# Output projection: a ninth of sixteen row-block pairs by seven products, final norm weights applied at the end, residual of three double groups added by DMA

## Chip, cores, metric

One core of one Trainium2 chip. The metric is the device time of one execution in microseconds (us), the median of several runs. The profile is of one execution, with the times of every instruction of the engines PE (matrix products), DVE (vector), ACT (scalar), POOL (GpSimd) and SP (which issues most DMAs).

## What is computed

One layer of a hybrid decoder for 256 tokens and 4096 channels, in float32. The normalised input is multiplied by one large input matrix, three branches (convolution, spatial gating, pooling) work on the parts, and their results, side by side, are `y`, 256 x 4096. The change is in what follows:

```python
    y = jnp.concatenate([ya, yb, yc], axis=-1) @ w_out[l]
    x = x + y
return _rmsnorm(x, final_g)      # x * rsqrt(mean(x*x) + eps) * final_g
```

So each output row needs its residual `x`, the sum of squares of the whole row, and at last a factor per row and a weight per column.

## The kernel before

Every float32 product is made from two parts of each operand: ACT casts a weight tile to a high part (line 237, `w_hi`), DVE subtracts it from the raw tile for a low part (line 238, `w_lo`), and PE does three matmuls of 128 x 128 x 512 for each block (high x high, high x low, low x high: lines 904 to 906 in the output projection, 357 to 359 elsewhere). A split tile has 1024 columns; five such slots go round, and PE uses a tile two tiles after it was split (`AHEAD`).

The output projection is the last stage. Its 4096 columns are done as four double groups of 1024 (`paired_columns`, g = 0, 2, 4, 6). The 4096 rows of `w_out` are 16 blocks p of 256 rows, taken in the order of `ORDER` (`LAST_ORDER` in the last double group). A block that is not in `PAIRED` ("plain") makes eight products: two token halves c, two column halves h, two row halves j. That is 24 matmuls from two split tiles. A block in `PAIRED` is done as a 2 x 2 x 2 block product by seven products, 21 matmuls, with sums of token blocks that were prepared before (`combos`) and sums of weight blocks that DVE makes on the way (lines 984, 987, 988, `w_sums`). It takes four splits with 3584 columns in all, in the order of products (1, 2), (3), (5, 7), (6, 4). The products add up in PSUM banks q1 to q8 over all 16 blocks.

When the last paired block of a double group is done, `between` combines q1, q5, q6 and q7 with one ACT copy and eight DVE sums of 512 columns, into the rows `xn`, which already hold the residual (`load_rows` loads it by SP at the fifth block of each double group, with 512 weights of the final norm for each half, `fg_bc`). When a bank of the plain products q2, q3, q4, q8 is complete, `rows_done` adds it to `xn` on DVE (line 893), ACT squares and sums the row (line 894) and DVE multiplies the norm weights in (line 899).

In the last double group the last five split tiles are held, and the second token half's products on them come last (30 matmuls). While these run, the first token half's rows are finished: `finish_rows` makes the row factor from the mean (DVE and ACT, lines 1022 to 1026), DVE multiplies the rows by it in five pieces (line 1031; the last 512 columns with their norm weights, line 1034), and SP writes each piece out (line 1035). Then the same is done for the second half.

The framework lists each engine's instructions itself: of those it thinks ready, the one written first goes first. So neighbouring instructions stand in an order a little different from the program's. Three raw tiles of 1 MB (`raw_tile`, tag `raw`) and two tiles of 4 x 512 columns (`scratch`, tag `sums`) go round in the last stage.

Of the kernel before, what the change touches and what calls it, by code (L numbers as in the profile page):

```python
# [28 lines left out]
P = 128  # L29
# [50 lines left out]

PAIRED = [5, 6, 7, 8, 9, 10, 11, 13]
ORDER = [0, 5, 1, 6, 2, 7, 8, 3, 9, 4, 10, 11, 12, 13, 14, 15]
LAST_ORDER = [0, 5, 1, 6, 2, 7, 8, 3, 9, 10, 4, 11, 13, 12, 14, 15]


PN = 0
# [9 lines left out]
def trunk(ctx: ExitStack, tc: tile.TileContext, x, xt, params, w1, wv, w2, w_pw, w_c, w_o, wst, bbias, blg, blb, fg, out):  # L98
# [777 lines left out]
        nc.scalar.activation(out=ssq[:, 0, 8:9], in_=ones[:, :1], func=AF.Sqrt)  # L876

    LAST = D - 512
    fg_bc = {}

    def load_rows(c0):
        at = len(traced())
        fg_bc[c0] = outp.tile([P, 512], F32, tag="fg", name="fg_bc", bufs=2)
        nc.sync.dma_start(out=fg_bc[c0], in_=fg[c0 : c0 + 512].partition_broadcast(P))
        nc.sync.dma_start(out=xn[:, :, c0 : c0 + 512], in_=x[:, c0 : c0 + 512].rearrange("(c p) d -> p c d", p=P))
        for ins in traced()[at:]:
            if ins.engine == mybir.EngineType.SP:
                tc.add_manual_dep(ins, last_load[0].name, ISSUE_ORDER, reason="behind the weights")

    def add_rows(c, ps, c0, w, i):  # L890

        z = xn[:, c, c0 : c0 + w]
        nc.vector.tensor_tensor(out=z, in0=ps, in1=z, op=ALU.add)  # L893
        nc.scalar.activation(out=ps, in_=z, func=AF.Square, accum_out=ssq[:, c, i : i + 1])
        return z

    def rows_done(c, ps, c0):
        z = add_rows(c, ps, c0, 512, c0 // 512)
        nc.vector.tensor_tensor(out=z, in0=z, in1=fg_bc[c0], op=ALU.mult)

    def product(q, a, w, j, f, l):

# [7 lines left out]
    def paired_columns(g, last=False):  # L910
# [18 lines left out]
        def plain(p, h, w):  # L929
            if (p, h) in holds:  # L930
                held.append((p, h, w))
            for c in range(1 if held else 2):
                for j in range(2):
                    into(PLAIN[c][h], y_hl[2 * p + j][:, c], w, j)
                if p == order[-1] and not held:
                    rows_done(c, q[PLAIN[c][h]], (g + h) * 512)

        def seven(p, products, w):
            i = PAIRED.index(p)
# [7 lines left out]
        def between():  # L947

            s = scratch("c_sums")
            v, y = s[:, 0], s[:, 1]  # L950
            x11, x12 = [xn[:, 0, (g + h) * 512 : (g + h + 1) * 512] for h in range(2)]
            x21, x22 = [xn[:, 1, (g + h) * 512 : (g + h + 1) * 512] for h in range(2)]
            nc.scalar.copy(out=v, in_=q[1])
            nc.vector.tensor_tensor(out=x11, in0=q[1], in1=x11, op=ALU.add)
            nc.vector.tensor_tensor(out=v, in0=q[6], in1=v, op=ALU.subtract)
            nc.vector.tensor_tensor(out=y, in0=q[5], in1=v, op=ALU.add)
            nc.vector.tensor_tensor(out=v, in0=q[7], in1=v, op=ALU.add)
            nc.vector.tensor_tensor(out=x22, in0=q[7], in1=x22, op=ALU.add)
            nc.vector.tensor_tensor(out=x21, in0=x21, in1=v, op=ALU.subtract)
            nc.vector.tensor_tensor(out=x12, in0=x12, in1=y, op=ALU.add)  # L960
            nc.vector.tensor_tensor(out=x22, in0=x22, in1=y, op=ALU.add)

        for n, p in enumerate(order):
            if g == 0 and n == 2:
                branches_done()
            if n == 4:
                load_rows(g * 512)
                load_rows((g + 1) * 512)
            raw = raw_tile("w_raw")
            for h in range(2):  # L970
                at = ((g + h) * 8 + p // 2) * P * 2048
# [21 lines left out]
            feed(*split(flat[:, 1024:]), lambda a, b, p=p: seven(p, (6, 4), (a, b)))  # L993
        if not last:
            return
        drain()
        rows_done(0, q[2], D - 1024)
        mean = mean_so_far(0, 7)
        add_rows(0, q[3], LAST, 512, 7)
        finish_rows(0, mean, 7, [1024, 1024, 1024, 512, 512])  # L1000
        for h in range(2):
            parts = [(p, w) for p, i, w in held if i == h]
            out_q = q[PLAIN[1][h]]
# [4 lines left out]
                rows_done(1, out_q, D - 1024)  # L1008
        mean = mean_so_far(1, 7)
        add_rows(1, out_q, LAST, 512, 7)  # L1010
        finish_rows(1, mean, 7, [512, 1024, 1024, 1024, 512])

    def mean_so_far(c, n):
        a = fin.tile([P, 1], F32, tag="fin_a", name="fin_a", bufs=2)
# [4 lines left out]
    def finish_rows(c, mean, i, pieces):  # L1019

        a, y, s = [fin.tile([P, 1], F32, tag=f"fin_{n}", name=f"fin_{n}", bufs=2) for n in "mys"]
        nc.vector.tensor_scalar(out=a, in0=ssq[:, c, i : i + 1], scalar1=1.0 / D, scalar2=mean, op0=ALU.mult, op1=ALU.add)
        nc.scalar.activation(out=s, in_=a, func=AF.Sqrt)
        nc.vector.reciprocal(out=y, in_=s)
        nc.vector.tensor_scalar(out=s, in0=y, scalar1=y, scalar2=a, op0=ALU.mult, op1=ALU.mult)
        nc.vector.tensor_scalar(out=s, in0=s, scalar1=-0.5, scalar2=1.5, op0=ALU.mult, op1=ALU.add)
        at = 0
        for w in pieces:
            z = xn[:, c, at : at + w]
            if at < LAST:  # L1030
                nc.vector.tensor_scalar(out=z, in0=z, scalar1=y, scalar2=s, op0=ALU.mult, op1=ALU.mult)  # L1031
            else:
                nc.vector.tensor_tensor(out=y, in0=y, in1=s, op=ALU.mult)
                nc.vector.scalar_tensor_tensor(out=z, in0=z, scalar=y, in1=fg_bc[LAST], op0=ALU.mult, op1=ALU.mult)
            nc.sync.dma_start(out=out[c * P : (c + 1) * P, at : at + w], in_=z)
            at += w

# [87 lines left out]
```

## Time and profile before

| | us |
|---|---|
| median of 3 runs | 1365.07 (1365.01 to 1366.15) |
| the profiled execution | 1364.61 |
| its span, first to last instruction | 1362.9 |
| output projection, first to last matmul | about 1022.6 to 1351.1 |

The span lies 1.7 us below the time of its execution, and that execution 0.5 us below the median. Of the span PE is busy for 99%, DVE for 78%, ACT for 51%; POOL for almost nothing. The page's second part shows PE at nine tenths or more in all but the last of 40 slices, at full granted clock, and DVE at nine tenths from slice 32 to the end.

### The profile page before, as it was taken

Reading aid. Unit: us, or ns where it says so; the run is one execution under the profiler, and the core shown is the slowest. Engines: PE = TensorE matmul, PEld = TensorE weight load, DVE = VectorE, ACT = ScalarE, POOL = GpSimd, SP = SyncE. Lnnn points to the kernel's source line nnn. Section 1 sums busy time; section 2 is a strip of 40 time slices with the busy share of each in tenths; the row PEclk is TensorE's granted clock in tenths of the full one; section 3 lists DMA queues with packets and bytes.
Section 4 is the critical chain, followed back from the end, with each engine's and each line's share of the span. In section 5 each row is a group of like instructions: output and inputs, shape, how many; then the busy total and the mean of one; then the engine's idle time right before and its main releaser. Section 6 shows DMA issues by size and latency. Waiting matters only on the chain.

```text
span 1362.9 us, 16202 instructions
## 1 busy us (share of the span) xinstructions
PE 1349.2 (99%) x6104; PEld 1120.1 (82%) x6104; DVE 1058.8 (78%) x1491; ACT 692.0 (51%) x837; POOL 5.8 (0%) x52
## 2 busy tenths in 40 slices
PE   9999999999999999999999999999999999999996
PEld 7888888888988888888888888888888888888885
DVE  7558888888888888777445844456878999999998
ACT  7653444435445434554344434446755665666563
POOL 0000000000000000000000000000000000000000
PEclk9999999999999999999999999999999999999998
DMA  9975555555556555555555555554736676666764
GB/s 333 351 263 192 198 185 187 193 193 199 185 200 196 195 203 187 186 187 187 182 185 186 190 202 195 185 189 147 248 123 233 217 251 216 221 223 213 243 220 156
DMA packets 58895, 281.01 MB, mean 206 GB/s; under 512 B 8896, under 2 KB 12352, under 8 KB 35520
## 3 DMA queue, kind: packets, MB, share of 16 engines
q1 hardware_dynamic: 58672, 279.95, 59.0%
q8 instruction: 48, 0.79, 0.2%
q14 instruction: 31, 0.25, 0.1%
q10 hardware_dynamic: 144, 0.02, 0.0%
HBM read 275.75 MB, written 4.19 MB: 205 GB/s over the span
## 4 chain that ended last, share of the span: by engine, by line
PE 97%; DVE 1%; DMA 1%; issue 0%; ACT 0%; SPq 0%; DVEq 0%
PE q L358 24%; PE q L359 24%; PE q L357 24%; PE q L905 8%; PE q L904 8%; PE q L906 8%; DMA gb<-in_blb_dram 1%; DMA x_raw<-in_xt_dram 0%; DVE xn L1031 0%; PE q L410 0%; PE q L632 0%; PE q L334 0%; DVE w_lo L238 0%; PE q L783 0%; DVE xn L893 0%
## 5 line engine op out<-in xcount | busy, mean ns | idle before, releaser
L238 DVE TENSOR_TENSOR w_lo<-w_raw,w_hi 128x1024 fp32r<-128x1024 f32 (+1 forms) x495 | 584.2, 1186 | 266.3 <-ACT w_hi L237 264.2
L237 ACT CAST w_hi<-w_raw 128x1024 fp32r<-128x1024 f32 (+1 forms) x495 | 501.8, 1023 | 528.2 <-PE q L359 306.6
L357 PE MATMUL q<-w_hi,act 128*128 128x512 f32 (+2 forms) x1504 | 578.9, 386 | 0.3 <-ACT act L314 0.3
L358 PE MATMUL q<-w_lo,act 128*128 128x512 f32 (+2 forms) x1504 | 577.4, 384 | 0.7 <-DVE w_lo L238 0.7
L359 PE MATMUL q<-w_hi,act 128*128 128x512 f32 (+2 forms) x1504 | 577.5, 384 | 0.0
L358 PEld LDWEIGHTS q<-w_lo,act 128*128 128x128 f32 x1504 | 282.9, 188 | 56.7 <-DVE w_lo L238 1.9
L359 PEld LDWEIGHTS q<-w_hi,act 128*128 128x128 f32 x1504 | 282.7, 188 | 55.3
L357 PEld LDWEIGHTS q<-w_hi,act 128*128 128x128 f32 x1504 | 282.8, 188 | 55.2 <-ACT act L314 0.8
L544 DVE SCALAR_TENSOR_TENSOR c_a<-h_a,par,c_a 128x256 f32<-128x256 f32 x360 | 153.6, 478 | 0.0
L905 PE MATMUL q<-w_lo,act 128*128 128x512 f32 x384 | 149.6, 390 | 0.0
L906 PE MATMUL q<-w_hi,act 128*128 128x512 f32 x384 | 149.3, 390 | 0.0
L904 PE MATMUL q<-w_hi,act 128*128 128x512 f32 x384 | 147.9, 390 | 0.0
L237 ACT CAST w_hi<-w_sums 128x1024 fp32r<-128x1024 f32 x64 | 67.4, 1053 | 71.9 <-DVE w_sums L988 44.3
L905 PEld LDWEIGHTS q<-w_lo,act 128*128 128x128 f32 x384 | 72.1, 188 | 15.5 <-DVE w_lo L238 0.5
L904 PEld LDWEIGHTS q<-w_hi,act 128*128 128x128 f32 x384 | 71.9, 188 | 15.3 <-ACT w_hi L237 0.4
L906 PEld LDWEIGHTS q<-w_hi,act 128*128 128x128 f32 x384 | 72.1, 188 | 14.9
L238 DVE TENSOR_TENSOR w_lo<-w_sums,w_hi 128x1024 fp32r<-128x1024 f32 x64 | 77.8, 1218 | 3.3 <-ACT w_hi L237 2.8
L984 DVE TENSOR_TENSOR w_sums<-w_raw 128x1024 f32<-128x1024 f32 x32 | 39.0, 1218 | 1.6 <-DMA w_raw<-in_w_o_dram 1.5
L905 PE MATMUL q<-w_lo,combo 128*128 128x512 f32 x96 | 37.6, 391 | 0.0
L906 PE MATMUL q<-w_hi,combo 128*128 128x512 f32 x96 | 37.4, 389 | 0.0
L904 PE MATMUL q<-w_hi,combo 128*128 128x512 f32 x96 | 37.4, 389 | 0.0
L988 DVE TENSOR_TENSOR w_sums<-w_sums,w_raw 128x512 f32<-128x512 f32 x32 | 21.9, 684 | 0.1
(143 smaller groups left out, 489.9 us busy)
## 6 DMA issues: line engine op xcount, KB each, us to landing
w_raw<-in_w_dram SPq DMA_DIRECT2D x149, 1024.0 KB, 4.8
w_raw<-in_w_o_dram SPq DMA_DIRECT2D x128, 512.0 KB, 4.9
w_raw<-in_wv_dram SPq DMA_DIRECT2D x20, 1024.0 KB, 4.8
w_raw<-in_w_pw_dram SPq DMA_DIRECT2D x9, 1024.0 KB, 4.9
x_rows<-in_x_dram SPq DMA_DIRECT2D x4, 1024.0 KB, 6.8
xn<-in_x_dram SPq DMA_DIRECT2D x8, 512.0 KB, 6.5
out_dram<-xn SPq DMA_DIRECT2D x6, 512.0 KB, 3.3
w_raw<-in_w_dram SPq DMA_DIRECT2D x5, 512.0 KB, 5.6
```

The lines of the kernel that those rows point to most:

```text
L237: nc.scalar.copy(out=hi[:, w], in_=raw[:, w])
L238: nc.vector.tensor_tensor(out=lo[:, w], in0=raw[:, w], in1=f32(hi[:, w]), op=ALU.subtract)
L357: nc.tensor.matmul(ps[:, :w], lhsT=act[:, c, 0], rhs=hi, start=f, stop=False)
L358: nc.tensor.matmul(ps[:, :w], lhsT=act[:, c, 0], rhs=lo, start=False, stop=False)
L359: nc.tensor.matmul(ps[:, :w], lhsT=act[:, c, 1], rhs=hi, start=False, stop=l)
L544: nc.vector.scalar_tensor_tensor(out=c_a[:, m], in0=src, scalar=w, in1=c_a[:, m], op0=ALU.mult, op1=ALU.add)
L904: nc.tensor.matmul(q, lhsT=a[:, 0], rhs=hi, start=f, stop=False)
L905: nc.tensor.matmul(q, lhsT=a[:, 0], rhs=lo, start=False, stop=False)
L906: nc.tensor.matmul(q, lhsT=a[:, 1], rhs=hi, start=False, stop=l)
L984: nc.vector.tensor_tensor(out=w57, in0=w[:, 0::3], in1=w[:, 2:3].broadcast_to([P, 2, 512]), op=ALU.add)
L988: nc.vector.tensor_tensor(out=s[:, 3], in0=s[:, 2], in1=w[:, 1], op=ALU.add)
```

## The change

- A ninth block, p = 12, is done by seven products in each double group. `ORDER` and `LAST_ORDER` are written anew: there are now seven plain blocks, and most paired blocks stand two in a row; in the last double group 11, 12 and 13 stand three in a row.
- The norm weights are no longer loaded for each half and multiplied in group by group. All 4096 are loaded in two DMAs of 1 MB into raw tiles behind the last weights, and `finish_rows` multiplies row factor and weights in by one scalar_tensor_tensor for each piece. The pieces are now 512, 512, 1024, 1024, 1024 for the first half and 512, 512, 1024, 1024, 512, 512 for the second.
- In the first three double groups the residual is no longer loaded into `xn`. `between` makes the combinations without it (two ACT copies, four DVE sums), `columns_done` adds each plain bank to them with one DVE sum, and POOL then issues a DMA that adds the residual from memory onto `xn` (four of 256 KB a double group). The squares of these rows are taken at the fourth block of the next double group, out of SBUF, into a `scratch` tile.
- In the last double group the residual is loaded and added as before.

```diff
-PAIRED = [5, 6, 7, 8, 9, 10, 11, 13]
-ORDER = [0, 5, 1, 6, 2, 7, 8, 3, 9, 4, 10, 11, 12, 13, 14, 15]
-LAST_ORDER = [0, 5, 1, 6, 2, 7, 8, 3, 9, 10, 4, 11, 13, 12, 14, 15]
+PAIRED = [5, 6, 7, 8, 9, 10, 11, 12, 13]
+ORDER = [0, 5, 1, 6, 7, 2, 8, 9, 3, 10, 11, 4, 12, 13, 14, 15]
+LAST_ORDER = [0, 5, 6, 1, 7, 8, 2, 9, 10, 3, 11, 12, 13, 4, 14, 15]
...
-    def load_rows(c0):
+    def load_rows(c0, residual):
         at = len(traced())
-        fg_bc[c0] = outp.tile([P, 512], F32, tag="fg", name="fg_bc", bufs=2)
-        nc.sync.dma_start(out=fg_bc[c0], in_=fg[c0 : c0 + 512].partition_broadcast(P))
-        nc.sync.dma_start(out=xn[:, :, c0 : c0 + 512], in_=x[:, c0 : c0 + 512].rearrange("(c p) d -> p c d", p=P))
+        if residual:
+            nc.sync.dma_start(out=xn[:, :, c0 : c0 + 512], in_=x[:, c0 : c0 + 512].rearrange("(c p) d -> p c d", p=P))
...
     def rows_done(c, ps, c0):
-        z = add_rows(c, ps, c0, 512, c0 // 512)
-        nc.vector.tensor_tensor(out=z, in0=z, in1=fg_bc[c0], op=ALU.mult)
+        add_rows(c, ps, c0, 512, c0 // 512)
...
                 if p == order[-1] and not held:
-                    rows_done(c, q[PLAIN[c][h]], (g + h) * 512)
+                    columns_done(c, h)
...
             nc.scalar.copy(out=v, in_=q[1])
-            nc.vector.tensor_tensor(out=x11, in0=q[1], in1=x11, op=ALU.add)
+            if last:
+                nc.vector.tensor_tensor(out=x11, in0=q[1], in1=x11, op=ALU.add)
+            else:
+                nc.scalar.copy(out=x11, in_=q[1])
+                y = x12
             nc.vector.tensor_tensor(out=v, in0=q[6], in1=v, op=ALU.subtract)
             nc.vector.tensor_tensor(out=y, in0=q[5], in1=v, op=ALU.add)
             nc.vector.tensor_tensor(out=v, in0=q[7], in1=v, op=ALU.add)
...
+            else:
+                nc.vector.tensor_tensor(out=x22, in0=q[7], in1=y, op=ALU.add)
+                z21.append(v)
...
+        def columns_done(c, h):
+
+            c0 = (g + h) * 512
+            z, r = xn[:, c, c0 : c0 + 512], q[PLAIN[c][h]]
+            if (c, h) == (1, 0):
+                nc.vector.tensor_tensor(out=z, in0=r, in1=z21[0], op=ALU.subtract)
+            else:
+                nc.vector.tensor_tensor(out=z, in0=r, in1=z, op=ALU.add)
+            nc.gpsimd.dma_start(out=z, in_=x[c * P : (c + 1) * P, c0 : c0 + 512], accum_op=ALU.add)
+            late_squares.append((c, c0))
+
         for n, p in enumerate(order):
...
+            while n == 3 and late_squares:
+                c, c0 = late_squares.popleft()
+                junk = scratch("junk")[:, 0]
+                nc.scalar.activation(out=junk, in_=xn[:, c, c0 : c0 + 512], func=AF.Square, accum_out=ssq[:, c, c0 // 512 : c0 // 512 + 1])
             if n == 4:
-                load_rows(g * 512)
-                load_rows((g + 1) * 512)
+                load_rows(g * 512, last)
+                load_rows((g + 1) * 512, last)
...
+        for at in (0, 2048):
+            fg_bc.append(raw_tile("fg_bc"))
+            nc.sync.dma_start(out=fg_bc[-1], in_=fg[at : at + 2048].partition_broadcast(P))
+            tc.add_manual_dep(traced()[-1], last_load[0].name, ISSUE_ORDER, reason="in the order of use")
...
-        finish_rows(0, mean, 7, [1024, 1024, 1024, 512, 512])
+        finish_rows(0, mean, 7, [512, 512, 1024, 1024, 1024])
...
-        finish_rows(1, mean, 7, [512, 1024, 1024, 1024, 512])
+        finish_rows(1, mean, 7, [512, 512, 1024, 1024, 512, 512])
...
+        nc.vector.tensor_tensor(out=y, in0=y, in1=s, op=ALU.mult)
         at = 0
         for w in pieces:
             z = xn[:, c, at : at + w]
-            if at < LAST:
-                nc.vector.tensor_scalar(out=z, in0=z, scalar1=y, scalar2=s, op0=ALU.mult, op1=ALU.mult)
-            else:
-                nc.vector.tensor_tensor(out=y, in0=y, in1=s, op=ALU.mult)
-                nc.vector.scalar_tensor_tensor(out=z, in0=z, scalar=y, in1=fg_bc[LAST], op0=ALU.mult, op1=ALU.mult)
+            g = fg_bc[at // 2048][:, at % 2048 : at % 2048 + w]
+            nc.vector.scalar_tensor_tensor(out=z, in0=z, scalar=y, in1=g, op0=ALU.mult, op1=ALU.mult)
             nc.sync.dma_start(out=out[c * P : (c + 1) * P, at : at + w], in_=z)
             at += w
```

## Rows read from the trace of the kernel before

**Rows 1.** The page, part 1 (busy us, share, instructions) and part 4 (chain).

```profile
PE 1349.2 (99%) x6104; PEld 1120.1 (82%) x6104; DVE 1058.8 (78%) x1491; ACT 692.0 (51%) x837; POOL 5.8 (0%) x52
...
PE 97%; DVE 1%; DMA 1%; issue 0%; ACT 0%; SPq 0%; DVEq 0%
```

**Rows 2.** Waits from 1000 to 1365 us: who waited for whom, total us, times, longest.

```profile
ACT w_hi L237 <- PE q L906: 53.7, 59, 2.6
...
DVE w_sums L984 <- DMA w_raw<-in_w_o_dram: 1.5, 2, 0.9
PEld q L905 <- DVE w_lo L238: 1.1, 3, 0.5
```

**Rows 3.** Timeline of PE: start us, us, engine, line; last double group's ends.

```profile
1269.15 0.39 PE L904 MATMUL q<-w_hi,act 128*128 128x512 f32 x1
...
1271.87 0.39 PE L904 MATMUL q<-w_hi,act 128*128 128x512 f32 x1
...
1350.89 0.39 PE L906 MATMUL q<-w_hi,act 128*128 128x512 f32 x1
```

**Rows 4.** Windows of 10 us: busy us (instructions) by engine, PEclk, DMA share, GB/s.

```profile
1310.00:1320.00 10.00, 10.00 (x46) 8.29 (x45) 10.00 (x11) 7.49 (x9) 0.00 (x0) 1.00 0.57 202
...
1340.00:1350.00 10.00, 9.97 (x45) 7.83 (x44) 8.66 (x18) 2.37 (x7) 0.00 (x0) 1.00 0.01 2
```

**Rows 5.** Groups by line and form, 1000 to 1365 us (busy us, mean ns, idle before).

```profile
L238 DVE TENSOR_TENSOR w_lo<-w_raw,w_hi 128x1024 fp32r<-128x1024 f32 x100 | 119.6, 1219 | 11.2 <-ACT w_hi L237 10.5
...
L984 DVE TENSOR_TENSOR w_sums<-w_raw 128x1024 f32<-128x1024 f32 x32 | 39.0, 1218 | 1.6 <-DMA w_raw<-in_w_o_dram 1.5
```

**Rows 6.** Timeline of DVE, three neighbours inside a paired block.

```profile
1326.58 1.22 DVE L238 TENSOR_TENSOR w_lo<-w_raw,w_hi 128x1024 fp32r<-128x1024 f32 x1
1327.72 0.68 DVE L987 TENSOR_TENSOR w_sums<-w_sums,w_raw 128x512 f32<-128x512 f32 x1
1328.32 0.68 DVE L238 TENSOR_TENSOR w_lo<-w_raw,w_hi 128x512 fp32r<-128x512 f32 x1
```

**Rows 7.** Timeline of DVE around and in the last double group.

```profile
1254.84 1.23 DVE L238 TENSOR_TENSOR w_lo<-w_raw,w_hi 128x1024 fp32r<-128x1024 f32 x1 [1.49 <-ACT w_hi L237]
...
1271.19 0.68 DVE L893 TENSOR_TENSOR xn<-q,xn 128x512 f32<-128x512 f32 x1
...
1301.86 1.22 DVE L238 TENSOR_TENSOR w_lo<-w_sums,w_hi 128x1024 fp32r<-128x1024 f32 x1
...
1341.28 2.35 DVE L238 TENSOR_TENSOR w_lo<-w_raw,w_hi 128x1024 fp32r<-128x1024 f32 x2
```

**Rows 8.** Timeline of DVE, the end: rows of both token halves finished.

```profile
1348.48 2.71 DVE L1031 TENSOR_SCALAR xn<-xn,fin_y,fin_s 128x1024 f32<-128x1024 f32 x4
...
1351.85 0.68 DVE L893 TENSOR_TENSOR xn<-q,xn 128x512 f32<-128x512 f32 x1
1352.44 0.74 DVE L1034 SCALAR_TENSOR_TENSOR xn<-xn,fin_y,fg_bc 128x512 f32<-128x512 f32 x1
1353.11 0.14 DVE L1016 TENSOR_SCALAR fin_a<-fin_a 128x1 f32<-128x1 f32 x1
...
1354.54 2.71 DVE L1031 TENSOR_SCALAR xn<-xn,fin_y,fin_s 128x512 f32<-128x512 f32 x4
...
1357.48 0.75 DVE L1034 SCALAR_TENSOR_TENSOR xn<-xn,fin_y,fg_bc 128x512 f32<-128x512 f32 x1
```

**Rows 9.** Timeline of SP: the last output DMA's issue.

```profile
1358.26 0.52 SPq L1035 DMA_DIRECT2D out_dram<-xn  x1
```

**Rows 10.** Windows of 2 us, columns as in rows 4.

```profile
1357.00:1359.00 2.00, 0.00 (x0) 0.00 (x0) 1.16 (x3) 0.00 (x0) 0.00 (x0) 0.50 1.02 408
```

**Rows 11.** The page, part 6: DMA issues, count, KB each, median us to landing.

```profile
xn<-in_x_dram SPq DMA_DIRECT2D x8, 512.0 KB, 6.5
...
fg_bc<-in_fg_dram SPq DMA_DIRECT2D x8, 256.0 KB, 4.5
...
out_dram<-xn SPq DMA_DIRECT2D x4, 256.0 KB, 3.1
```

More of the change, by code (lines that the diff above doesn't have):

```diff
@@ L878, in trunk @@
     LAST = D - 512
-    fg_bc = {}
-    def load_rows(c0):
+    fg_bc = []
+    late_squares = deque()
+    def load_rows(c0, residual):
         at = len(traced())
-        fg_bc[c0] = outp.tile([P, 512], F32, tag="fg", name="fg_bc", bufs=2)
-        nc.sync.dma_start(out=fg_bc[c0], in_=fg[c0 : c0 + 512].partition_broadcast(P))
-        nc.sync.dma_start(out=xn[:, :, c0 : c0 + 512], in_=x[:, c0 : c0 + 512].rearrange("(c p) d -> p c d", p=P))
+        if residual:
+            nc.sync.dma_start(out=xn[:, :, c0 : c0 + 512], in_=x[:, c0 : c0 + 512].rearrange("(c p) d -> p c d", p=P))
         for ins in traced()[at:]:
@@ L957, in between @@
             nc.vector.tensor_tensor(out=v, in0=q[7], in1=v, op=ALU.add)
[L958 to L961, printed above, removed]
+            if last:
+                nc.vector.tensor_tensor(out=x22, in0=q[7], in1=x22, op=ALU.add)
+                nc.vector.tensor_tensor(out=x21, in0=x21, in1=v, op=ALU.subtract)
+                nc.vector.tensor_tensor(out=x12, in0=x12, in1=y, op=ALU.add)
+                nc.vector.tensor_tensor(out=x22, in0=x22, in1=y, op=ALU.add)
+            else:
+                nc.vector.tensor_tensor(out=x22, in0=q[7], in1=y, op=ALU.add)
+                z21.append(v)
+        z21 = []
+        def columns_done(c, h):
[7 more added lines that the diff above has]
+            late_squares.append((c, c0))
         for n, p in enumerate(order):
```

## Prediction

> **What bounds the kernel now.** I read the page first: PE is busy for 99% of the span and carries 97% of the chain that ended last; POOL does almost nothing [rows 1]. The waits say whether PE is ever short of work in the last stage: of its waits only 1.1 us, three times, are for a split tile (w_lo), while ACT waits 53.7 us for PE to free a slot [rows 2]. PE's own timeline gives the price of a matmul: twelve between 1269.15 and 1271.87, so 0.2267 us, and the last double group's 360 take 1269.15 to about 1351.1, 0.4 us more than 360 x 0.2267 [rows 3]. So what leaves PE leaves the span, if nothing takes its place. The windows name what may: DVE is busy 10.00 of 10 us at 1310, and PE is still whole there; in 1340 to 1350, at the end of the loop, it is 9.97 [rows 4]. Two engines run level, and the change moves work between them.
>
> **PE.** A seventh product instead of an eighth saves 3 matmuls a double group, 12 in all: 12 x 0.2267 = -2.72 us. That is the whole of what the change can take from PE.
>
> **DVE's budget.** A split of 1024 columns and the first weight sum take 1.22 us each [rows 5], but start 1.14 us apart, and ones of 512 columns 0.60 [rows 6]; I count these pitches. A paired block is 4 x 1.14 + 3 x 0.60 = 6.36 us on DVE against 21 x 0.2267 = 4.76 on PE; a plain one 2.28 against 5.44. Each of the first three double groups had 8 x 6.36 + 8 x 2.28 + 16 sums x 0.60 = 78.7 us on DVE; it will have 9 x 6.36 + 7 x 2.28 + 8 x 0.60 = 78.0, since four combinations, four norm products go and the residual moves to DMAs. PE goes from 81.6 to 80.9. The spare time stays 2.9 us, so these groups should run at PE's pace. ACT gets one copy and 1.5 split tiles more, some 2.2 us a group, beside an idle quarter [rows 4].
>
> **DVE in the last double group.** Here the combinations stay. Up to the held matmuls DVE goes from 73.9 to 78.0 us and PE from 74.8 (330) to 74.1 (327). What counts is by how much a split is ready ahead of its product. Take it at the last tile of block 13 of the third group, and follow it to the last tile of the last group. Before: DVE does 2 plain blocks, 16 sums and 73.9, together 88.1, PE 378 matmuls, 85.7: it loses 2.4 us. After: 2 plain blocks, 8 sums and 78.0, 87.4, against 375 matmuls, 85.0: 2.4 again. But the starting value falls. Before, DVE had caught up there: it waited 1.49 us for a cast at 1254.84, so block 13's last split was done by 1253.4, and its product starts 54 matmuls before 1269.15, at 1256.9: 3.5 us ahead [rows 7]. In the new order 12 and 13 are paired in a row, each costing 1.6 us of the lead. Where two stood in a row before, the last tile of block 8 was done at 1301.86 + 1.14 = 1303.0 and its product, 150 matmuls after 1269.15, starts at 1303.15: 0.15 us ahead [rows 7]. At best the slot binds: it is freed 21 matmuls (4.76 us) ahead, and cast and split take 2.3, so 2.5 us. So we start 1.0 to 2.5 us ahead (1.0 because the lighter boundary returns some of it) instead of 3.5. At the end the old kernel was already late: its last splits ran from 1341.28 to 1343.6, and by count the last tile's products start 35 matmuls ahead of 1350.89, at 1343.0, so 0.6 late. After, with up to 1.7 us of DVE idleness on the way (as before) or none, the end lies between 0.1 ahead and 3.1 late. Against 0.6 that is -0.6 to +2.5 us of PE waiting. I take the middle, +0.9, because three paired blocks in a row (11, 12, 13) draw on the lead just before the end.
>
> **The tail.** The row of events: DVE scales the first half's rows from 1348.48; the sum of the last bank starts at 1351.85, the second half's scaling at 1354.54, and it ends at 1358.23 [rows 8]; the last output DMA is issued at 1358.26 [rows 9], and the span ends at 1362.9, 4.67 later, with the DMA engines full (share 1.02, 408 GB/s at 1357 to 1359 [rows 10]). A scaling with weights over 512 columns takes 0.67 us to the next start (1352.44 to 1353.11); for 1024 I take 0.67 + 0.54 = 1.21, the step that splits show; 2 x 0.67 bounds it above. The first half: 2 x 0.67 + 3 x 1.21 = 4.97, from 1348.6 (the small multiply, 0.15, now comes first) to 1353.6. If the last bank's sum is listed behind it, it starts 1.75 late; the second half's scaling starts 2.84 later, 1356.4, and takes 4 x 0.67 + 2 x 1.21 = 5.1: DVE ends at 1361.5. The columns now come at 256 KB each 0.67 us, 391 GB/s, less than the 408 that the DMAs moved, so the last piece finds short queues: 3.1 us to landing [rows 11] and the 0.7 that the old span had after its slowest landing, so 1365.3: +2.4. If the sum is listed first, pieces of the first half fill the gaps of the row factor's chain and delay it by about 0.7: DVE ends at 1360.3, the span at 1364.1: +1.2. I take the middle, +1.8. The four norm products that leave the loop's last group were only partly on this path, so I credit nothing.
>
> **The accumulating DMAs.** No DMA of POOL is in this trace. The nearest rows: 256 KB land in 3.1 us (output) or 4.5 (weights), 512 KB of residual in 6.5 [rows 11]. An accumulation reads twice and writes once; I take 6.5, with 3.1 and 13 as bounds. Their cover: the last bank's sum of a double group starts 2.0 us after the next has begun (1271.19), so that DMA leaves about 2.7 us in. The squares stand on ACT behind the second cast of block 1, whose slot frees after 30 matmuls, 6.8 us in, so the fourth square comes about 10 us in. So 6.5 us hide, by 0.8. Queued behind a late one are the casts of the next paired block on ACT, and its weight sum on DVE, since the squares' output takes turns with that tile. PE is some 1.0 us ahead there; each further us costs one in each of three groups. Gone are the loads of the residual and weights in these groups, behind which DVE waited 1.5 us for raw tiles [rows 2]; PE did not feel it, so I count zero, and a gain at most inside the 0.9 above. The two loads of 1 MB take raw tiles of blocks 4 and 14; the second is free around 1338 to 1340 and lands some 6.5 us later, at most 1347, before 1348.6. SP stands in its wait for that tile, but behind it are only output DMAs. If this cover fails, the third and later pieces wait for as long.
>
> On the accumulating DMAs the Trainium skill speaks against the change (SBUF — State Buffer, SBUF: two separate sides): a DMA issued from GpSimd has its descriptors written by that engine, which is locked out while DVE runs in a two-port mode. It names copies, casts and tensor_scalar for that, and tensor_tensor as having no such mode. No run here shows a DMA from POOL; by that rule the loop's DVE work, all TENSOR_TENSOR in rows 5 to 7, would leave the sum as it is.
>
> **Sum.** -2.72 + 0.9 + 1.8 = 0.0 against the profiled 1364.61 (span 1362.9 and 1.7 around it); the median lies 0.5 above, so 1365.1.
>
> **Rivals.** (1) The gain arrives: the pieces fall into gaps, DMA engines still set the end (2 MB at 408 GB/s is 5.1 us from the first piece at 1355.4, so the end moves by about -0.3), and the lead holds (-0.6): -2.72 - 0.3 - 0.6 = -3.6, or -2.7 with one of them: 1361.5 to 1362.4. For it: the end was DMA-bound; against it: DVE must do some 3 us more there. (2) Slower, by accumulating DMAs: with DVE always busy [rows 4] POOL may be slow to issue, or four of them stand in line. From 8.3 us to landing PE waits; at 11 it is some 2 us in each of three groups, so +6: 1371. For it: nothing in the trace covers this form; against it: 0.8 us of cover, DMA share 0.57. (3) Slower, by DVE's debt in the last double group: squares that wait for weight-sum tiles of block 6 hold back ACT, and the lead is used up before 11, 12, 13: +2.5 for the lead and +2.4 for the tail, and 1 to 2 of waits: 1367.3 to 1369.
>
> **Chances.** A measurement tells about 0.2%, 2.7 us, from no change. Forecast, inside that: 0.54 (1362.6 to 1367.6). Rival 1: 0.18. Rival 2: 0.12, rival 3: 0.16, of which a little falls inside; slower 0.27, same 0.55. The range 1361.8 to 1369.3 leaves out half of rival 2 and a part of rival 1.
>
> **What would show it.** 1428 matmuls in the projection in place of 1440; waits of PE for w_lo of a few us, most of them at the end of the last group; DVE's last scaling ending about 3 us later after the last matmul; squares on ACT without a wait for DMA. I am wrong if PE waits in the first three groups, or if the first half's scaling no longer precedes the last bank's sum.

## The result, and the profile after

The changed kernel takes 1376.63 us (median of 4 runs, 1375.79 to 1379.24) against 1365.04 for the kernel before beside it: a ratio of 1.0087, 95% interval 1.0076 to 1.0099, so 11.6 us slower. The forecast was 1365.1 with a range up to 1369.3; the time lies 7.3 us above the range.

The profiled execution of after is the one of 1375.79 us, span 1374.1, which is 11.2 more than before. Three stretches add up to that. The output projection begins 1.0 us earlier (1021.55 for 1022.59). From its first matmul to its last (called the projection below) it takes 336.23 us (1021.55 to 1357.78) where it took 328.30: +7.9, although it has 12 matmuls fewer. From the start of the last matmul to the end of the span (called the tail) it takes 16.3 us where it took 12.0: +4.3.

From the page of after: part 1 (busy us, share, instructions), part 3 (DMA queues: packets, MB, share of the 16 engines' span), part 4 (chain) and part 6 (issues: count, KB each, median us to landing).

```profile
PE 1349.5 (98%) x6092; PEld 1119.2 (81%) x6092; DVE 1064.0 (77%) x1490; ACT 701.9 (51%) x851; POOL 16.2 (1%) x64
...
q1 hardware_dynamic: 56320, 276.80, 57.4%
q0 software_dynamic: 1728, 3.15, 1.3%
...
PE 84%; issue 7%; DVE 5%; DMA 3%; ACT 1%; POOL 0%; DVEq 0%; SPq 0%; ACTq 0%; POOLq 0%
...
xn<-in_x_dram POOLq DMA_DIRECT2D x12, 256.0 KB, 8.1
```

PE does 12 matmuls fewer (6092 for 6104) and is busy just as long (1349.5 for 1349.2, [rows 1]), although the span grew by 11.2. Its share of the chain falls from 97% to 84%; that is what one path, followed back, ran through, and not how long PE stood. What came into the chain are DMAs, DVE and the gaps between them. The accumulating DMAs are the 12 of POOL: 8.1 us to landing, where the prediction took 6.5.

The waits of after from 1000 to 1376 us (who waited for whom: us in total, times, longest), as [rows 2] has them for before:

```profile
ACT junk L990 <- DMA xn<-in_x_dram: 12.7, 8, 6.4
...
PEld q L905 <- DVE w_lo L238: 6.0, 8, 1.6
DVE w_sums L1009 <- ACT junk L990: 4.8, 2, 4.5
PEld q L904 <- ACT w_hi L237: 4.3, 1, 4.3
...
PE q L904 <- ACT w_hi L237: 3.9, 1, 3.9
```

The squares (junk) wait for the accumulating DMAs, eight times and once for 6.4 us; DVE's weight sums wait for the squares; PE waits for a cast. Before had neither of the first two waits, and of the third only one of 0.4 us, by PE's weight load. Where it happens, the windows of 10 us say (busy us and instructions of PE, PEld, DVE, ACT, POOL; granted clock; DMA share; GB/s):

```profile
1100.00:1110.00 10.00, 10.00 (x46) 8.27 (x45) 7.70 (x10) 2.25 (x4) 3.59 (x4) 1.00 0.89 220
1110.00:1120.00 10.00, 5.42 (x18) 3.81 (x17) 5.39 (x5) 6.41 (x12) 0.00 (x0) 0.80 0.55 158
1120.00:1130.00 10.00, 10.00 (x39) 8.07 (x39) 9.74 (x12) 4.47 (x6) 0.00 (x0) 0.86 0.65 211
```

This is the start of the second double group, which by count begins at 1103.87 (39 matmuls before 1112.71). In the first window ACT works 2.25 us of 10 and DVE 7.70, in the second PE works 5.42. ACT's timeline there shows what it stands in:

```profile
1101.35 0.62 ACT L237 CAST w_hi<-w_raw 128x512 fp32r<-128x512 f32 x1 [1.66 <-PE q L906]
1108.38 0.63 ACT L990 ACTIVATE junk<-xn 128x512 f32<-128x512 f32 x1 [6.40 <-DMA xn<-in_x_dram]
...
1109.01 1.03 ACT L237 CAST w_hi<-w_sums 128x1024 fp32r<-128x1024 f32 x1
...
1115.08 0.63 ACT L990 ACTIVATE junk<-xn 128x512 f32<-128x512 f32 x1 [1.86 <-DMA xn<-in_x_dram]
...
1115.70 1.03 ACT L237 CAST w_hi<-w_sums 128x1024 fp32r<-128x1024 f32 x1
```

ACT's first square is next in line at 1101.97, before the group has even begun, and stands until 1108.38. Behind it are the last casts of block 5, of summed tiles (w_sums). The chain, which ends in PE's second wait there, goes by the other route, from the last square to a weight sum on DVE; its pieces in order (start, us, what):

```profile
1104.44 0.61 POOL xn L981
1105.06 9.94 DMA xn<-in_x_dram
...
1115.61 0.20 ACT junk L990
1115.83 0.97 DVE w_sums L1009
...
1116.97 1.23 DVE w_lo L238
1118.24 0.79 PE q L905
```

And PE's timeline, at this place, at the start of the third group, and its last matmul:

```profile
1112.48 0.39 PE L906 MATMUL q<-w_hi,act 128*128 128x512 f32 x1
1116.78 0.79 PE L904 MATMUL q<-w_hi,combo 128*128 128x512 f32 x1 [3.91 <-ACT w_hi L237]
1118.24 0.79 PE L905 MATMUL q<-w_lo,combo 128*128 128x512 f32 x1 [0.67 <-DVE w_lo L238]
1118.83 0.63 PE L906 MATMUL q<-w_hi,combo 128*128 128x512 f32 x1
...
1122.67 0.48 PE L906 MATMUL q<-w_hi,act 128*128 128x512 f32 x1
1123.00 0.40 PE L904 MATMUL q<-w_hi,act 128*128 128x512 f32 x1
...
1203.84 0.50 PE L905 MATMUL q<-w_lo,act 128*128 128x512 f32 x1 [0.84 <-DVE w_lo L238]
...
1217.55 0.50 PE L905 MATMUL q<-w_lo,combo 128*128 128x512 f32 x1 [1.18 <-DVE w_lo L238]
...
1357.78 0.39 PE L906 MATMUL q<-w_hi,act 128*128 128x512 f32 x1
```

At PE's pace the matmul of 1118.24 would have started at 1112.48 + 2 x 0.2267 = 1112.93: 5.3 us lost to waiting. From 1118.24 to 1123.00 eleven matmuls take 4.76 us instead of 2.49: 2.3 us more, lost to the clock, as the section on the hardware shows. That is 7.6 us at one place. The third group adds 0.84 + 1.18 = 2.0, the fourth 0.4 (the window 1330 to 1340, PE 9.62). Together 10.0 of the 10.6 by which the projection is longer than in before, once the 12 matmuls that it lacks are counted in (7.9 + 2.7).

The second wait, for w_lo, comes by way of DVE: its weight sum could not start before the last square was done, since both write tiles of the same two. What each route, the casts behind the squares and the tiles, would cost without the other, no run separates.

The place of the squares differs from group to group, although it is written once. In the third group one cast of block 5 stands behind the first three of them. In the fourth, whose `LAST_ORDER` has two paired blocks ahead of its fourth block, all casts of block 5 are ahead of them:

```profile
1281.92 1.06 ACT L237 CAST w_hi<-w_raw 128x1024 fp32r<-128x1024 f32 x1 [1.66 <-PE q L906]
1282.88 0.62 ACT L990 ACTIVATE junk<-xn 128x512 f32<-128x512 f32 x1
```

There the DMAs land latest of all (8.3 to 11.6 us after their issue; 7.0 to 9.9 at the second group, 5.1 to 7.0 at the third), and PE loses least.

The tail, on DVE's timeline of after, to be read beside [rows 8]:

```profile
1353.45 0.69 DVE L894 TENSOR_TENSOR xn<-q,xn 128x512 f32<-128x512 f32 x1 [0.44 <-PE q L906]
...
1357.05 5.00 DVE L1061 SCALAR_TENSOR_TENSOR xn<-xn,fin_y,fg_bc 128x512 f32<-128x512 f32 x5
1361.97 0.68 DVE L894 TENSOR_TENSOR xn<-q,xn 128x512 f32<-128x512 f32 x1
...
1364.81 5.13 DVE L1061 SCALAR_TENSOR_TENSOR xn<-xn,fin_y,fg_bc 128x512 f32<-128x512 f32 x6
```

The last bank's sum starts 4.19 us after the last matmul's start (1361.97 - 1357.78); before it was 0.96 (1351.85 - 1350.89). That is +3.2. From that sum to the scaling 2.84 for 2.69: +0.15. The scaling 5.13 for 3.69 (1354.54 to 1358.23): +1.4. From DVE's end to the span's end 4.16 for 4.67: -0.5. Sum +4.3.

### The profile page after: what moved, and what is told of

Same layout as the page of the kernel before. It is cut to its first block, busy times and chain, and to the rows that moved or that the text cites. A ratio compares the mean times of both kernels' runs of the same rounds, so it can differ in the third digit from the quotient of the medians.

```text
span 1374.1 us, 16232 instructions
## 1 busy us (share of the span) xinstructions
PE 1349.5 (98%) x6092; PEld 1119.2 (81%) x6092; DVE 1064.0 (77%) x1490; ACT 701.9 (51%) x851; POOL 16.2 (1%) x64
## 3 DMA queue, kind: packets, MB, share of 16 engines
q0 software_dynamic: 1728, 3.15, 1.3%
HBM read 275.75 MB, written 4.19 MB: 204 GB/s over the span
## 4 chain that ended last, share of the span: by engine, by line
PE 84%; issue 7%; DVE 5%; DMA 3%; ACT 1%; POOL 0%; DVEq 0%; SPq 0%; ACTq 0%; POOLq 0%
PE q L358 24%; PE q L359 24%; PE q L357 24%; PE q L905 4%; PE q L906 4%; PE q L904 4%; DVE w_lo L238 3%; DMA xn<-in_x_dram 2%; DVE w_sums L1009 1%; DMA gb<-in_blb_dram 1%; DVE xn L1061 1%; ACT w_hi L237 0%; DMA w_raw<-in_w_dram 0%; PE q L410 0%; PE q L632 0%
## 5 line engine op out<-in xcount | busy, mean ns | idle before, releaser
L905 PE MATMUL q<-w_lo,act 128*128 128x512 f32 x368 | 144.1, 392 | 0.8 <-DVE w_lo L238 0.8
L906 PE MATMUL q<-w_hi,act 128*128 128x512 f32 x368 | 143.8, 391 | 0.0
L904 PE MATMUL q<-w_hi,act 128*128 128x512 f32 x368 | 142.0, 391 | 0.0
L237 ACT CAST w_hi<-w_sums 128x1024 fp32r<-128x1024 f32 x72 | 75.8, 1053 | 62.5 <-DVE w_sums L1013 28.0
L238 DVE TENSOR_TENSOR w_lo<-w_sums,w_hi 128x1024 fp32r<-128x1024 f32 x72 | 86.9, 1217 | 9.9 <-ACT w_hi L237 9.8
L906 PEld LDWEIGHTS q<-w_hi,act 128*128 128x128 f32 x368 | 69.5, 189 | 14.3
L1009 DVE TENSOR_TENSOR w_sums<-w_raw 128x1024 f32<-128x1024 f32 x36 | 43.8, 1217 | 6.1 <-ACT junk L990 4.8
L904 PE MATMUL q<-w_hi,combo 128*128 128x512 f32 x108 | 42.4, 393 | 3.9 <-ACT w_hi L237 3.9
L905 PE MATMUL q<-w_lo,combo 128*128 128x512 f32 x108 | 43.1, 399 | 2.2 <-DVE w_lo L238 2.2
L906 PE MATMUL q<-w_hi,combo 128*128 128x512 f32 x108 | 42.3, 392 | 0.0
L905 PEld LDWEIGHTS q<-w_lo,combo 128*128 128x128 f32 x108 | 20.4, 189 | 8.7 <-DVE w_lo L238 4.7
```

What stands on the lines that cost most here:

```text
L237: nc.scalar.copy(out=hi[:, w], in_=raw[:, w])
L238: nc.vector.tensor_tensor(out=lo[:, w], in0=raw[:, w], in1=f32(hi[:, w]), op=ALU.subtract)
L904: nc.tensor.matmul(q, lhsT=a[:, 0], rhs=hi, start=f, stop=False)
L905: nc.tensor.matmul(q, lhsT=a[:, 0], rhs=lo, start=False, stop=False)
L906: nc.tensor.matmul(q, lhsT=a[:, 1], rhs=hi, start=False, stop=l)
L1009: nc.vector.tensor_tensor(out=w57, in0=w[:, 0::3], in1=w[:, 2:3].broadcast_to([P, 2, 512]), op=ALU.add)
```

## The experiments

My theory after this: the squares stand at the wrong place on ACT and wait there for DMAs, and that is the larger part of the loss; the rest lies in the tail. The rivals: the accumulating DMAs cost through the DMA engines whatever waits for them; or the ninth pair overloads DVE. Times are medians and ratios are against the kernel before, run beside each; projection and tail are of the one profiled execution.

**The squares later.** At the ninth block of the order instead of the fourth, nothing else.

```diff
-            while n == 3 and late_squares:
+            while n == 8 and late_squares:
```

> The changed kernel, but the squares of a double group's rows are taken at the ninth block of the next double group instead of the fourth. Theory A: the changed kernel's time comes from two places, 9.6 us of PE waiting and slow clock behind casts that stand on ACT behind squares that wait for accumulating DMAs, and 4.3 us in the tail. Then the PE waits of 3.9 us near 1113 and of 0.8 and 1.2 us near 1205 go, the last matmul comes about 8 us sooner (near 1350) and the time is 1368 (1367 to 1369.5); the tail stays at 16 us behind the last matmul. Rival B: DVE has too much work with nine pairs, the squares only show it. Then PE waits as long, in other places, and the time stays within 2 us of 1376.6.

Measured: 1368.66 us (1366.89 to 1369.65), ratio 1.0027 [1.0015, 1.0039]; the projection takes 328.01 (1022.47 to 1350.48) instead of 336.23, the tail 15.8. That is theory A, with 8.0 us of the 11.6 for the place of the squares. No square waits for a DMA any more, and in the window that was worst PE is nearly whole, at full clock:

```profile
1110.00:1120.00 10.00, 9.68 (x43) 7.71 (x42) 8.12 (x9) 5.06 (x6) 0.00 (x0) 1.00 0.86 234
```

But the loop is not at its 323.7 (1428 x 0.2267): it is 4.3 above, where before was 1.9 above its own 326.4. DVE now waits for raw tiles of the weights, of which PE feels 0.3 us at this place; and the last bank's sum starts 3.7 us behind the last matmul. DVE's timeline, at both:

```profile
1111.88 1.23 DVE L1009 TENSOR_TENSOR w_sums<-w_raw 128x1024 f32<-128x1024 f32 x1 [2.17 <-DMA w_raw<-in_w_o_dram]
...
1354.21 0.68 DVE L894 TENSOR_TENSOR xn<-q,xn 128x512 f32<-128x512 f32 x1
```

**Copies instead of accumulations.** The squares stand at their early place again. The sum with the products is left out, so only the times count.

```diff
-            nc.gpsimd.dma_start(out=z, in_=x[...], accum_op=ALU.add)
+            nc.gpsimd.dma_start(out=z, in_=x[...])
```

> The changed kernel, but POOL's DMAs copy the residual over the rows instead of adding it: the sum with the product is left out, so only its times count. Landing of POOL's DMAs was 8.1 us in the median. If the addition in the DMA costs that, landing falls to 3 to 5 us, the squares do not wait, PE's wait of 3.9 us goes, and the time is 1368 to 1371. If it is POOL's issue and the queue, landing stays at 7 to 8 us and the time at 1375 to 1378.

Measured: 1368.59 us (one run), projection 328.56, tail 16.3. From its page (queue; issues) and its windows:

```profile
q0 software_dynamic: 960, 3.15, 0.7%
...
xn<-in_x_dram POOLq DMA_DIRECT2D x12, 256.0 KB, 5.6
```

```profile
1110.00:1120.00 10.00, 9.06 (x40) 7.21 (x39) 7.94 (x9) 7.47 (x13) 0.00 (x0) 1.00 0.47 147
```

Landing falls from 8.1 to 5.6 us, the squares' longest wait from 6.4 to 3.7, and PE's long wait and the low clock are gone, though the squares stand where they stood. The time is the one expected for that, but not the landing (3 to 5 us), and the squares still wait 7.3 us in all: PE still waits 0.9 us for a split at 1114. So the larger part of the loss needs both: the early place and the 2.5 us by which an accumulation lands later than a copy. The queue lines fit that: for the same 3.15 MB the accumulations' packets take 1.3% of the DMA engines' span and the copies' 0.7%.

**Loads for the accumulations, nine pairs kept.** The residual is loaded and added as before, in all groups.

```diff
-                    columns_done(c, h)
+                    rows_done(c, q[PLAIN[c][h]], (g + h) * 512)
...
-                load_rows(g * 512, last)
+                load_rows(g * 512, True)
```

> The changed kernel with the residual loaded by SP and added on DVE in all four double groups, as before the change; nine pairs, the new orders and the norm weights at the end stay. DVE then has 9 x 6.36 + 7 x 2.28 + 12 x 0.60 = 80.4 us a double group against 80.9 on PE. Theory A (squares behind accumulating DMAs): PE waits 1 to 3 us in all, the last matmul comes near 1349 to 1351, and with the tail of 16 us the time is 1367 to 1369. Rival B (DVE's debt): with four more sums a group PE waits more than in the changed kernel, and the time is 1377 or above.

Measured: 1367.87 us (1366.06 to 1372.55), ratio 1.0025 [1.0015, 1.0035]; projection 328.44, tail 16.7. Its profiled execution is the longest of its runs and lost some 3 us in an earlier stage, so only these stretches are read from it. This is theory A again; rival B, at 1377 or above, is out. Without any accumulating DMA the kernel is still slower than before by 0.25%: ninth pair and end weights together don't pay either.

**The weights at the end alone.** Eight pairs, the old orders, loads; of the change only the final norm's weights in the last scaling.

```diff
-PAIRED = [5, 6, 7, 8, 9, 10, 11, 12, 13]
+PAIRED = [5, 6, 7, 8, 9, 10, 11, 13]
...
```

> The kernel before with one part of the change alone: the norm weights come in at the end, with the new pieces; eight pairs, the old orders, the residual loaded. It measures the tail by itself. If the 4.3 us of the tail come from the longer scaling and from the last bank's sum being listed behind it, the time is 1365.0 + 3.5 to 4.5 = 1368.5 to 1369.5, with the last matmul where it was (1350.9). If they come from the debt that nine pairs leave on DVE at the end, it is 1366 to 1367.5.

Measured: 1365.52 us (1364.82 to 1366.32), ratio 1.0003 [0.9994, 1.0013]; projection 327.19, tail 13.84. DVE's timeline at its end:

```profile
1346.44 5.00 DVE L1061 SCALAR_TENSOR_TENSOR xn<-xn,fin_y,fg_bc 128x512 f32<-128x512 f32 x5
...
1351.43 0.68 DVE L894 TENSOR_TENSOR xn<-q,xn 128x512 f32<-128x512 f32 x1
...
1354.27 5.13 DVE L1061 SCALAR_TENSOR_TENSOR xn<-xn,fin_y,fg_bc 128x512 f32<-128x512 f32 x6
```

The first half's scaling starts 2.8 us before the last matmul (1349.26 by PE's timeline), as it did in the kernel before (2.4), and the tail grows by 1.8. The loop gives 1.1 of it back (327.19 for 328.30), so the time lies below both expectations, nearer to the second (the debt of nine pairs). The loads experiment differs from this one by the ninth pair and its orders alone and takes 1367.87: with 12 matmuls less it is 2.35 us slower. Its tail of 16.7 has no accumulation either, so the other 2.5 us of after's tail (16.3 - 13.8) come with the ninth pair. The ninth pair alone, with the weights left in the loop, was not tried.

**The last bank's sum first.** As the first experiment, and the first half's scaling is written behind the sum of the last bank.

```diff
-        finish_rows(0, mean, 7, [512, 512, 1024, 1024, 1024])
...
         add_rows(1, out_q, LAST, 512, 7)
+        finish_rows(0, first_mean, 7, [512, 512, 1024, 1024, 1024])
```

> The kernel with late squares, with the scaling of the first token half's rows written behind the sum of the last bank, so that this sum is listed ahead of what is left of the scaling. With late squares alone the sum starts 3.7 us after the last matmul begins, behind five scalings. Theory A (the order of the list makes the longer scaling a delay): the sum starts within 1 us of the last matmul, the left-over scalings fill the gaps of the second row factor, and 1.5 to 3 us come back: 1365.7 to 1367.2. Rival B (DVE's work or the output DMAs set the end, whatever the order): the same within 0.7 us, 1368 to 1369.3.

Measured: 1367.68 us (1365.49 to 1369.70), ratio 1.0020 [1.0011, 1.0030], for 1.0027 without it: about 1 us, between the two expectations, and the intervals overlap. The tail is 14.9 for 15.8. DVE's timeline:

```profile
1352.71 0.68 DVE L894 TENSOR_TENSOR xn<-q,xn 128x512 f32<-128x512 f32 x1
1353.31 2.47 DVE L1061 SCALAR_TENSOR_TENSOR xn<-xn,fin_y,fg_bc 128x1024 f32<-128x1024 f32 x2
...
1357.07 5.13 DVE L1061 SCALAR_TENSOR_TENSOR xn<-xn,fin_y,fg_bc 128x512 f32<-128x512 f32 x6
```

The sum starts 1.3 us after the last matmul (1351.38) instead of 3.7. But the two pieces of the first half that were left, 2.47 us, now run while ACT takes the last squares, and hold back the factor: from the sum to the scaling 4.36 us instead of 2.85. Of the 2.4 us that the sum gains, 1.5 go there.

**The same with eight pairs and loads** (the weights at the end, and the sum first).

> Eight pairs, old orders, loaded residual, norm weights at the end, and the sum of the last bank ahead of the first half's scaling. Against the same without that (1365.5): there the sum starts 2.2 us after the last matmul begins. Theory A: 1 to 1.5 us less, 1364 to 1364.5, as the kernel before or a little faster, because the loop lost four norm products a group and PE's waits went from 1.9 to 0.8 us. Rival B (DVE or DMA bound at the end): 1365.5, no change.

Measured: 1364.71 us (1363.93 to 1367.23), ratio 1.0000 [0.9991, 1.0009]; projection 327.16, tail 13.06: 1.05 above before, where the prediction had +1.2 for this listing. The gain against the same with the sum behind (ratio 1.0003) is within the intervals.

**Nine pairs in three groups, eight in the last.** On top of the kernel with late squares and the sum first. Here block 12's operand stays in its combined form in the last group, so what is computed there is changed.

```diff
-LAST_ORDER = [0, 5, 6, 1, 7, 8, 2, 9, 10, 3, 11, 12, 13, 4, 14, 15]
+LAST_ORDER = [0, 5, 1, 6, 2, 7, 8, 3, 9, 10, 4, 11, 13, 12, 14, 15]
...
+        paired = [p for p in PAIRED if not (last and p == 12)]
```

> Nine pairs in the first three double groups with accumulating DMAs and late squares; eight pairs and the old order in the last; sum of the last bank first. PE has 9 matmuls less than before, 2.0 us. Theory C (the nine-pair order of the last double group leaves DVE late, so that the first half's rows are done 1 to 2 us later relative to the last matmul): the tail is 13 us or less behind the last matmul as with eight pairs, and the time is 1363 to 1365. If the accumulating DMAs' own load (raw tiles 2.2 us late behind them) is what costs, PE still waits 2 us or more in the first three groups, and it is 1365 to 1367.

Measured: 1364.92 us (1363.53 to 1366.45), ratio 1.0001 [0.9992, 1.0010], for 1.0020 with nine pairs in the last group, on the same chip: 2.8 us by the medians, although PE has 3 matmuls more (0.7 us). The projection takes 327.97 for 329.51, the tail 13.6 for 14.9 (theory C had 13 or less). So in the last group the ninth pair, with the order that goes with it, costs some 3.5 us and saves 0.7.

**The same with loads.**

> The same with the residual loaded by SP and added on DVE in all groups: nine pairs in the first three, eight in the last, sum of the last bank first. DVE has 80.4 of 80.9 us in each of the first three groups. If that is enough, 1363 to 1365, and no accumulating DMA is needed for nine pairs; if a full DVE loses time at each group's end, PE waits for casts and splits for 2 to 4 us and the time is 1365 to 1367.

Measured: 1362.39 us (1361.85 to 1363.92), ratio 0.9985 [0.9976, 0.9994]; projection 326.82, tail 13.0. Two comparisons on this chip. Against the kernel above, which differs in the accumulating DMAs and their late squares alone: 2.5 us less by the medians, so these cost that even where no square waits for a DMA. Against eight pairs everywhere: 1362.39 for 1364.71, 2.3 us less, and nine matmuls are 2.04. So the seven products do give their matmuls back, in the groups where DVE has the time. This holds for a kernel that, like the one above, doesn't make block 12's operand whole for the last group.

**That version with the whole computation.** Block 12's operand is made whole again by four small sums and a copy at the start of the last group, and the first half's scaling is cut the other way round.

```diff
+            if last and n == 2:
+                whole_block_again()
...
-        finish_rows(0, first_mean, 7, [512, 512, 1024, 1024, 1024])
+        finish_rows(0, first_mean, 7, [1024, 1024, 1024, 512, 512])
```

> Nine pairs in the first three double groups and eight in the last, residual loaded everywhere, norm weights at the end, sum of the last bank first; before the last double group block 12's first-row operand is made whole again from its prepared form (four small DVE sums and a small cast, some 1.1 us), and the first half's pieces are 1024, 1024, 1024, 512, 512. The run with eight pairs in the last group left that out and took 1362.4. If the small sums hide (DVE has room at that boundary, since four norm products left it), 1362 to 1363; if not, PE waits about 1 us more and it is 1363 to 1364. The kernel before is 1364.7.

Measured: 1364.20 us (1362.68 to 1365.68), ratio 0.9992 [0.9983, 1.0001]; projection 325.46, tail 13.5. That is slower than either expectation, and not told apart from the kernel before. The loop is down by 2.8 us from before's 328.30, and the tail takes 1.5 of that back. PE does not wait for the small sums: by its timeline nothing is lost at the last group's start, and the projection is 1.4 us shorter than in the run above.

**The accumulating DMAs by themselves.** Eight pairs and the old orders, weights at the end, sum first, late squares: the sixth experiment with accumulating DMAs in three groups. (By the prediction's pitches DVE has 73.9 us to do in each of these, not 72.)

> Eight pairs in the old orders, norm weights at the end, sum of the last bank first, and the residual by accumulating DMAs with late squares in three double groups. With the residual loaded the same took 1364.7. Theory: accumulating DMAs delay raw tiles by some 2 us at each group's start, which PE feels only where DVE has no spare time; with eight pairs DVE has 72 of 81.6 us to do, so PE does not wait and the time is 1364 to 1365.2. Rival: they cost by themselves, in PE waits of 1 us or more a group, and it is 1366 to 1368.

Measured: 1366.03 us (1365.05 to 1369.27), ratio 1.0009 [1.0000, 1.0018], for 1.0000 [0.9991, 1.0009] with loads. The intervals overlap, so by itself this is no proof; the sign is that of the pair before, and the projection is 1.2 us longer (328.36 for 327.16), the tail 0.6 (13.7 for 13.06). The time is at the edge of the rival's, but without its waits: PE does not wait in the first three groups. It loses time in the last one, near 1341, 60 us after the last accumulation landed. What comes between stands on the timelines of ACT and DVE:

```profile
1294.97 0.64 ACT L990 ACTIVATE junk<-xn 128x512 f32<-128x512 f32 x1 [2.64 <-DVE w_lo L238]
```

```profile
1296.66 1.83 DVE L238 TENSOR_TENSOR w_lo<-w_raw,w_hi 128x1024 fp32r<-128x1024 f32 x2 [1.13 <-ACT w_hi L237]
```

A late square waits, no longer for a DMA, but for DVE to be done with one of the two tiles that squares and weight sums share; then DVE waits for the casts behind it. In this kernel the squares wait 6.6 us so, three times. From 1265 to 1352 us DVE stands 4.4 us for casts and raw tiles, in the sixth experiment 0.7. That this is the whole price was not tested: no run gives the squares a tile of their own.

Over the three pairs that differ in this alone the accumulations with their squares cost 0.3 us (late squares: ratios 1.0027 and 1.0025), 1.2 and 2.2 (by the ratios). They never gained.

## Why the prediction was wrong

**The step that failed** is the cover of the accumulating DMAs: "The squares stand on ACT behind the second cast of block 1 ... so the fourth square comes about 10 us in. So 6.5 us hide, by 0.8." The place was wrong: it was taken from the program's order, and no row showed it. At the second group the squares are listed ahead of the last casts of block 5, and ACT comes to the first one 1.9 us before the group begins, not several us in. There was no cover but a debt from the first square on. Why the framework lists them so early there is not shown. The landing time was the smaller miss: 8.1 us in the median for 6.5, inside the bounds of 3.1 to 13, the last one of this boundary 9.9. Neither would have cost PE 5 us alone: with late squares the 7.9 us of landing are hidden, and with copies at the early place 5.6 us of landing leave PE 9.06 of 10.

**Rival 2 was the case in the main** (slower by the accumulating DMAs, chance 0.12), though at 1371 it was 5.6 us short. Its threshold of 8.3 us of landing for PE to wait rested on the same cover and was too high: copies that land in 5.6 us in the median still make PE wait. Its price was too even: 2 us in each of three groups (2.7 by its own rule of a us for each us above 8.3), where the trace has 7.6, 2.0 and 0.4. In the fourth group's boundary the squares fall behind casts that were wanted earlier and hardly wait (0.8 us for a DMA there). And it had nothing for the clock, 2.3 us of the 7.6. Parts of rival 3 came true beside it: squares that wait for weight-sum tiles, seen in the last experiment, and a debt in the last group that reaches the tail. The prediction had the rivals as alternatives, and none of its times added them up. Of the two signs that would show me wrong, the first appeared, waits of PE ahead of the last group. The second did not: the first half's scaling still precedes the last bank's sum, and now all five pieces of it stand in that sum's way.

**PE, -2.72: right.** 1428 matmuls; and 2.3 us came back from nine of them where nothing else took them. **DVE's budget in the first three groups: right** as far as the pairs go: in that run, with the residual loaded and 80.4 us for DVE, PE loses 1.2 us there beyond the start that all runs share, all of it between 1046 and 1065.

**DVE in the last group, +0.9 (-0.6 to +2.5): right mechanism, mis-sized.** After's last splits are two from 1349.22, done at 1351.5, and the last tile's product would start at 1349.85 by PE's timeline: 1.65 late, inside the 0.1 ahead to 3.1 late that the step counted. But little of it shows as waiting of PE. PE took held products first, and the first half's banks came later: the sum of 1353.45 lies 4.3 us ahead of the last matmul, where before's lay 5.7 ahead (1345.19). So the first half's scaling starts 0.73 us before the last matmul instead of 2.4, and runs into the last bank's sum. The two experiments with the last group at nine and eight pairs price the whole at about 3.5 us, of which 2.2 in the loop (329.51 - 327.97 + 0.7) and 1.3 in the tail. I had looked for this debt in PE's waits only, and had put the tail on a schedule that the debt moves.

**The tail, +1.8 (+1.2 to +2.4): right, with the old start.** The scalings of the two halves took 5.00 and 5.13 us for 4.97 and 5.1. With the weights alone the tail is 13.84 for 12.01, +1.8; that this is the middle of the range is luck, since the sum stood behind the scaling there, for which the step had +2.4, and the first half began 2.8 us ahead of the last matmul, not the 2.3 of the step. With the sum first it is +1.05 for +1.2. In the changed kernel the term is 4.3, because the step took 1348.6 for the start of the first half, from the kernel before.

**What the 11.6 us are made of**, by the runs: squares at the early place 8.0; the sum behind the scaling 1.0; the ninth pair in the last group 2.8; accumulating DMAs with their squares 2.5. These are steps between the medians of kernels that follow one on another, and add to 14.3; what is left, nine pairs in three groups with the weights at the end, is 2.3 below the kernel before (1362.39 for 1364.72). That 14.3 - 2.3 = 12.0 comes near the 11.6 is no check, since the steps run from one end to the other; the rest is chips and noise. Each price holds at its place in the row: the accumulations with their squares cost 2.5 here, and 0.3 with the ninth pair in the last group. With block 12 made whole again what is left is 0.9 (1364.20 for 1365.07). The two ratios, 0.9985 and 0.9992, have overlapping intervals, and the pieces of the scaling were changed in the same run; PE's timeline shows no price of the four sums and the copy, and what else would make a difference stays open.

## What to carry to other kernels

An instruction that waits for a transfer must be listed behind everything that its engine owes before the transfer can have landed: here one index of a loop, three or eight, decided 8 us. Find its place by what the engine has been handed already when it is listed, not by the program's order of blocks. And when a step takes an engine's lead at the end of a loop, look for the cost in what that engine does after the loop too.

## What the runs showed of the hardware

**TensorE's clock after a gap.** Windows of 2 us of after (columns as above):

```profile
1116.00:1118.00 2.00, 0.79 (x1) 0.29 (x1) 2.00 (x2) 2.00 (x3) 0.00 (x0) 0.51 0.00 0
1118.00:1120.00 2.00, 1.76 (x4) 1.47 (x5) 2.00 (x3) 2.00 (x3) 0.00 (x0) 0.50 0.00 0
...
1124.00:1126.00 2.00, 2.00 (x11) 1.63 (x10) 1.95 (x3) 1.06 (x1) 0.00 (x0) 1.00 0.64 172
```

After PE had stood from 1112.7 to 1116.8 the granted clock is 0.50, the level of 1.2 GHz; the matmuls from 1118.83 to 1122.67 come every 0.427 us (nine in 3.84). At 1123.00 the next ones come 0.23 apart again, and the granted clock of 1124 to 1126 is 1.00, 2.4 GHz. So the wait's own 5.3 us drew 2.3 more behind it. The waits of 0.84 and 1.18 us in the third group left no such trace: the windows around them have clock 1.00.

**An accumulating DMA takes about twice a copy's time on the DMA engines.** By the two pages, 1.3% of the span for 0.7%, for the same bytes; at the second group's start (1100 to 1116 us), by the queue lines of after and then of the kernel with copies (packets, MB, share):

```profile
q0 software_dynamic: 576, 1.05, 37.7%
```

```profile
q0 software_dynamic: 320, 1.05, 20.0%
```

The weights feel it: four loads of 512 KB issued there land in 7.8 us in the median beside accumulations, 5.8 beside copies. The issue of one takes POOL 0.86 us in the median for an accumulation and 0.54 for a copy, by POOL's timeline.

The Trainium skill (DMA: Bandwidth & Descriptors, Anatomy of one DMA — SWDGE (gpsimd) path) gives a fit for such a DMA, 2.0 us and the bytes over 436e3 per us, which for 256 KB is an estimate of 2.6 us. The 5.6 of a copy and 8.1 of an accumulation, beside a stream of weights with a DMA share of 0.88 and 0.89 (1100 to 1110 us), are not described by it.

What the prediction weighed from the Trainium skill (SBUF — State Buffer, SBUF: two separate sides) is not contradicted: the issues took 0.84 to 1.13 us beside DVE's TENSOR_TENSOR. No run here sets another kind of DVE work against it.
